# A three-block network in one launch: queries of the first attention padded by map, its small loads moved to SyncE, and the second pool gate moved behind mixing

## The chip, the cores and the metric

The kernel runs on one core of a Trainium2 chip. The metric is device time in microseconds for one execution. Engines are called TensorE (PE, with its weight loads as PEld), VectorE (DVE), ScalarE (ACT), GpSimd (POOL) and SyncE (SP).

## The reference

One input of 256 tokens by 1024 features goes through two blocks of a first network and one block of a second. What matters here is the first network's start:

```python
def adaln_params(cond, w_mod, b_mod):
    m = jax.nn.silu(cond) @ w_mod + b_mod
    return jnp.split(m, N_MOD, axis=-1)          # shift, scale, gate, twice

# block 0: differential attention, 8 heads of 2 maps x 64, latents (256) attend to context + latents (512)
hx, hc = modulate(x, sh1, sc1), modulate(h_ctx, csh1, csc1)
k_c, v_c = project_kv(hc, w_qkv)
q_l = apply_rope(project_q(hx, w_qkv), cos, sin)
k_l, v_l = project_kv(hx, w_qkv);  k_l = apply_rope(k_l, cos, sin)
s = jnp.einsum('bqhmd,bkhmd->bhmqk', q * (HEAD_DIM ** -0.5), k)   # m: the two maps
p = jax.nn.softmax(s, axis=-1)
a = p[:, :, 0] - lam * p[:, :, 1]
o = jnp.einsum('bhqk,bkhe->bqhe', a, v)
...
# block 1: pooled means over windows of 2, 4, 8, 16 tokens, then a matmul for each group
y = jnp.einsum('bsgi,gio->bsgo', pooled, w_pool).reshape(B, S, D)
y_lat = y * pool_scale
# both blocks
x = layer_norm(ALPHA * x + g1 * y_lat, ln_g[i, 0], ln_b[i, 0])
x = layer_norm(ALPHA * x + g2 * swiglu(modulate(x, sh2, sc2), ffn_w_in, ffn_w_out), ln_g[i, 1], ln_b[i, 1])
```

The second network's block (three attention branches and an FFN) follows and isn't touched.

## The kernel before

All matrix products with large weights run as three matmuls in fp32r: each operand is split in a high part and a low remainder, and `mm3` (lines 77 to 80) adds high x high, high x low and low x high. Weights come from HBM by SyncE into four `raw` buffers; `wsplit` lets ScalarE cast a half of a unit (line 70) and VectorE subtract (line 71). PSUM has four banks called mm, two called tp (transposes) and two called s (`sbank`). A tile framework orders the instructions of each engine before the launch from its own estimates: it takes what is ready and comes first in the program, and `behind(ins)` only adds the rule that what the block holds stands behind `ins` where both are on one engine.

**The modulation stream.** The modulation vectors of the later stages come from 4 MB slices of w_mod. `mod_stream` is a generator: one step (`mod_step`) loads 512 KB by GpSimd (line 131, three `mraw` buffers) and lets VectorE multiply it by the condition and add it to `acc` (line 132). Eight steps make a group. Behind the eighth, TensorE sums `acc` over partitions, into columns (line 138) or, for a gate, into rows with two matmuls by a matrix of ones (line 145), which ScalarE copies back (line 146). The groups come in the order f0 (two groups), g1_0, p (two), f1 (two), g2_0, g1_1, g2_1; `mod_until(key)` runs steps until that key is there. The layer norm's rows (`ln_rows`, line 345) and `pool_scale` use the same `mraw` buffers.

**The first attention.** The first modulation comes in four quarters q: `load_quarter` issues two pieces of w_mod, the columns of x and ctx and the rows of w_qkv for the first head pair on SyncE's queue; `mod_quarter` and `modulate` make the modulated, transposed hT (latents) and hc (context); `Chunk.products` adds the quarter's part of keys, queries and values of head pair 0. `rest(q)` holds the products that come later, the last being `rest(3)`. Then come, behind the last modulation activation (`seq["mod"]`, line 567), ScalarE's DMA issues for prow (norm gains in rows), rope (the tables) and lamr (lines 642 to 658), the transpose of prow (line 648) and the small sums for lambda. For each of four head pairs g: `rope_T` rotates keys and then queries on VectorE (lines 684 to 687), transposes them (line 690) and splits them in high and low parts (`split_to`, lines 673 and 674). The two maps of a head lie on partitions 0 to 63 and 64 to 127. `scores` makes one set of scores for one query tile and one head:

```python
for i, (q, k) in enumerate(((qh, kh), (qh, kl), (ql, kh))):
    for m in range(2):
        p = slice(m * 64, (m + 1) * 64)
        with behind(*last):
            last = pe.matmul(Sm[m], q[p, h, tk], k[p, h, :], start=i == 0, stop=i == 2).ins,
```

So each matmul reads 64 partitions, and maps alternate. VectorE takes minima (line 708), ScalarE exponentials (line 710), VectorE mixes the maps (line 713), TensorE transposes (line 717). After each of the four sets two modulation steps stand behind the mixing. The projections of the next head pair are what TensorE does meanwhile.

**The pool stage.** The first FFN takes three modulation steps for each pair of hidden tiles and one for each unit of its output, which leaves two steps of g1_1. `mod_until("g1_1")` runs these, then `psg` is loaded and multiplied with the gate's rows (lines 839 to 841), then the FFN's held-back output products go through the norm n2 (line 254 and on), are mixed over tokens by matmuls (line 837) and scaled and shifted into T (line 870); `project_T` multiplies by the pool's weights (line 882), and the norm n3 multiplies the product by psg. The bias table of the second network (`bias_tables`, line 159) is filled by GpSimd at the start of this stage.

## Time and profile before

| | |
|---|---|
| median of 3 runs | 1156.4 us (1154.62 to 1157.67) |
| profiled execution | 1157.81 us, of which the span of the trace is 1156.0 us |
| TensorE busy | 1129.1 us (98% of the span) |
| VectorE busy | 829.0 us (72%) |
| ScalarE busy | 575.8 us (50%) |
| mean granted TensorE clock | 0.995 of full speed |

Busy time is the time in which an engine has an instruction of its own under way; register, semaphore and DMA-issuing instructions don't count. Matmuls overlap: each record is longer than the distance to the next one, so the cost of a stream of matmuls is read from starts. The granted clock is the share of TensorE's full 2.4 GHz; 0.50 is the other level, 1.2 GHz.

### The profile page before, as it was taken

How to read it: one execution, taken by the hardware profiler on the slowest of the kernel's cores; microseconds unless marked ns; L12 is line 12 of the kernel's file. 1: busy time of each engine (PE TensorE's matmuls, PEld its weight loads, DVE VectorE, ACT ScalarE, POOL GpSimd, SP SyncE). 2: the span in 40 equal slices, each digit the busy share in tenths (PEclk: the TensorE clock that was granted, in tenths of full speed). 3: DMA queues.
4: the chain of work that ended last, by engine and by line, in shares of the span. 5: the costliest groups of instructions: out<-in, count | busy, mean ns of one | idle time of the engine just before them, and what ended most of it. 6: DMA issues, size and time to landing. Idle time of an engine off the chain costs nothing. (4 is left out here: it accounts for less than half of the span.)

```text
span 1156.0 us, 19870 instructions
## 1 busy us (share of the span) xinstructions
PE 1129.1 (98%) x7967; PEld 1035.3 (90%) x7967; DVE 829.0 (72%) x1547; ACT 575.8 (50%) x1017; POOL 83.9 (7%) x154
## 2 busy tenths in 40 slices
PE   8989999999999999999999889999999999999998
PEld 7979988889999877999988779989999989999986
DVE  5677887887887877856654779788788674655541
ACT  5643444576444436654543655455346356545430
POOL 0101110100111111000000020000100000000000
PEclk9999999999999999999999999999999999999999
DMA  9956545648998993867565353660456254664530
GB/s 311 324 174 212 183 155 174 219 146 285 313 317 291 341 353 121 249 217 257 210 222 175 109 180 121 179 200 29 146 160 223 77 178 147 219 199 167 215 113 37
DMA packets 149098, 229.69 MB, mean 199 GB/s; under 512 B 5708, under 2 KB 121051, under 8 KB 149006
## 3 DMA queue, kind: packets, MB, share of 16 engines
q1 hardware_dynamic: 133440, 176.10, 46.6%
q0 software_dynamic: 14672, 50.63, 13.0%
q10 hardware_dynamic: 894, 1.69, 0.5%
q8 instruction: 63, 1.03, 0.4%
q14 instruction: 29, 0.24, 0.1%
HBM read 226.36 MB, written 2.04 MB: 198 GB/s over the span
## 5 line engine op out<-in xcount | busy, mean ns | idle before, releaser
L71 DVE TENSOR_TENSOR wlo<-raw,whi 128x1024 fp32r<-128x1024 f32 (+2 forms) x318 | 372.7, 1193 | 135.2 <-ACT whi L70 133.7
L70 ACT CAST whi<-raw 128x1024 fp32r<-128x1024 f32 (+2 forms) x318 | 316.3, 1028 | 229.6 <-PE mm L80 86.7
L78 PE MATMUL mm<-hTh,whi 128*128 128x256 f32 x1056 | 299.1, 283 | 0.0
L80 PE MATMUL mm<-hTh,wlo 128*128 128x256 f32 x1056 | 298.9, 283 | 0.0
L79 PE MATMUL mm<-hTl,whi 128*128 128x256 f32 x1056 | 298.3, 282 | 0.0
L79 PEld LDWEIGHTS mm<-hTl,whi 128*128 128x128 f32 x1056 | 199.4, 189 | 0.3
L78 PEld LDWEIGHTS mm<-hTh,whi 128*128 128x128 f32 x1056 | 199.3, 189 | 0.3
L80 PEld LDWEIGHTS mm<-hTh,wlo 128*128 128x128 f32 x1056 | 199.3, 189 | 0.1
L78 PE MATMUL mm<-whi,hTh 128*128 128x256 f32 (+4 forms) x592 | 185.5, 314 | 2.3 <-DVE hTh L336 1.8
L80 PE MATMUL mm<-whi,hTl 128*128 128x256 f32 (+4 forms) x592 | 184.8, 313 | 0.4 <-DVE hTl L337 0.4
L79 PE MATMUL mm<-wlo,hTh 128*128 128x256 f32 (+4 forms) x592 | 184.3, 312 | 0.6 <-DVE wlo L71 0.6
L78 PEld LDWEIGHTS mm<-whi,hTh 128*128 128x128 f32 x592 | 112.4, 190 | 9.0 <-DVE hTh L336 2.9
L79 PEld LDWEIGHTS mm<-wlo,hTh 128*128 128x128 f32 x592 | 112.3, 190 | 4.9 <-DVE wlo L71 1.0
L80 PEld LDWEIGHTS mm<-whi,hTl 128*128 128x128 f32 x592 | 111.9, 189 | 5.2 <-DVE hTl L337 1.0
L132 DVE SCALAR_TENSOR_TENSOR acc<-mraw,csil,acc 128x1024 f32<-128x1024 f32 x80 | 102.2, 1280 | 10.0 <-DMA mraw<-in_w_mod_dram 9.6
L78 PE MATMUL mm<-whi,hid 128*128 128x512 f32 x264 | 104.3, 395 | 0.0
L79 PE MATMUL mm<-wlo,hid 128*128 128x512 f32 x264 | 104.2, 395 | 0.0
L80 PE MATMUL mm<-whi,hid 128*128 128x512 f32 x264 | 103.7, 393 | 0.0
L131 POOL DMA_DIRECT2D mraw<-in_w_mod_dram x80 | 42.6, 533 | 367.8 <-DVE acc L132 269.8
L79 PEld LDWEIGHTS mm<-wlo,hid 128*128 128x128 f32 x264 | 49.6, 188 | 11.6 <-issue 1.0
L80 PEld LDWEIGHTS mm<-whi,hid 128*128 128x128 f32 x264 | 49.6, 188 | 11.5 <-issue 0.7
L78 PEld LDWEIGHTS mm<-whi,hid 128*128 128x128 f32 x264 | 49.6, 188 | 11.4 <-issue 0.7
(329 smaller groups left out, 1556.6 us busy)
## 6 DMA issues: line engine op xcount, KB each, us to landing
raw<-in_ffn_w_in_dram SPq DMA_DIRECT2D x44, 1024.0 KB, 7.1
mraw<-in_w_mod_dram POOLq DMA_DIRECT2D x80, 512.0 KB, 5.0
raw<-in_ffn_w_out_dram SPq DMA_DIRECT2D x22, 1024.0 KB, 4.9
raw<-in_w_ffn_in_dram SPq DMA_DIRECT2D x22, 1024.0 KB, 5.2
raw<-in_w_in_dram SPq DMA_DIRECT2D x16, 1024.0 KB, 5.5
raw<-in_w_ffn_out_dram SPq DMA_DIRECT2D x11, 1024.0 KB, 5.0
raw<-in_w_in_dram SPq DMA_DIRECT2D x14, 768.0 KB, 4.4
raw<-in_attn_w_qkv_dram SPq DMA_DIRECT2D x9, 1024.0 KB, 8.4
```

The lines of the kernel that those rows point to most:

```text
L70: se.copy(hv[:, sl], raw[:, sl])
L71: seq["sub"] = ve.tensor_sub(lv[:, sl], raw[:, sl], hv[:, sl].bitcast(F32)).ins
L78: pe.matmul(o, lh, rh, start=first, stop=False, **kw)
L79: pe.matmul(o, lh, rl, start=False, stop=False, **kw)
L80: return pe.matmul(o, ll, rh, start=False, stop=last, **kw).ins
L131: gp.dma_start(raw, wv[:, k, g * 1024:(g + 1) * 1024])
L132: ve.scalar_tensor_tensor(acc, raw, csil[:, k, 0:1], acc, op0=ALU.mult, op1=ALU.add)
```

## The change

The queries of a head pair lie in two tiles QZ (high and low part) with one plane for each map; the partitions of the other map are zeros that GpSimd writes once. A score matmul then reads all 128 partitions of queries and keys, and the set runs map by map, three matmuls each. The query split is done for 64 partitions at a time. Two of the eight modulation steps of a head pair stand behind the query rotation, one behind the mixing of each set, two ahead of the head output. The small loads (prow, rope, lamr) are issued by SyncE behind the last load of quarter 3, and their users stand behind `rest(3)` and the last fill of weights. In the pool stage the last steps of g1_1, its sums and psg stand behind mixing.

```diff
--- before.py
+++ after.py
@@ -25,7 +25,7 @@
 QS = -0.125
 HALF = (slice(0, 512), slice(512, 1024))
 
-STEPS_S, STEPS_IN, STEPS_OUT = 2, 3, 1
+STEPS_S, STEPS_IN, STEPS_OUT = 1, 3, 1
 
 
 @with_exitstack
@@ -523,7 +523,7 @@
             rw = wp.tile([128, 2048], F32, tag="raw", name="raw", bufs=4)
             rw = rw[:, :1536].rearrange("p (w k c) -> p w k c", w=3, k=2)
             for i, kind in enumerate((1, 0, 2)):
-                sp.dma_start(rw[:, i], wq[:, 2 * q:2 * q + 2, kind * 1024:kind * 1024 + 256])
+                seq["ld"] = sp.dma_start(rw[:, i], wq[:, 2 * q:2 * q + 2, kind * 1024:kind * 1024 + 256]).ins
                 if i == 1:
                     load_x("ctx", q)
             return raws, rw
@@ -603,11 +603,12 @@
                         tk = slice(t * 128, (t + 1) * 128)
                         for k in ks:
                             if self.kind == 1:
-                                mm3(self.PC[:, t, :], wh[:, k, tk], wl[:, k, tk], hc[0][:, k, :], hc[1][:, k, :],
+                                i = mm3(self.PC[:, t, :], wh[:, k, tk], wl[:, k, tk], hc[0][:, k, :], hc[1][:, k, :],
                                     k == 0 and t == 0, k == 7, **kw)
                             else:
-                                mm3(self.PC[:, t, :], hc[0][:, k, tk], hc[1][:, k, tk], wh[:, k, :], wl[:, k, :],
-                                    k == 0 and t == 0, k == 7, **kw)
+                                i = mm3(self.PC[:, t, :], hc[0][:, k, tk], hc[1][:, k, tk], wh[:, k, :], wl[:, k, :],
+                                        k == 0 and t == 0, k == 7, **kw)
+                    return i
 
         ALLK = range(8)
         ck, cq, cv = (Chunk(kind, 0) for kind in (1, 0, 2))
@@ -616,11 +617,25 @@
         def rest(q):
             ks = range(2 * q, 2 * q + 2)
             cv.products(ks, con=False)
-            ck.products(ks, lat=False)
+            seq["rest"] = ck.products(ks, lat=False)
 
         for q in range(4):
             with behind(*((first_dma.ins,) if not q else ())):
                 raws, rw = load_quarter(q)
+            if q == 3:
+
+                with behind(seq["ld"]):
+                    prow = cp.tile([128, 128], F32, name="prow")
+                    gp.memset(prow, 0.0)
+                    sp.dma_start(prow[32:64], I["ln_g"].rearrange("l w (k c) -> (l w k) c", c=128))
+                    sp.dma_start(prow[64:96], I["ln_b"].rearrange("l w (k c) -> (l w k) c", c=128))
+                    sp.dma_start(prow[96:104], rows128(I["norm1_g_2"][0]))
+                    sp.dma_start(prow[104:112], rows128(I["norm2_g_2"][0]))
+                    sp.dma_start(prow[112:113], I["attn_subln_g"])
+                    rope = at.tile([128, 2, 2, 2, 64], F32, name="rope")
+                    sp.dma_start(rope, I["k_rope"].rearrange("(t p) v w c -> p t v w c", p=128))
+                    lamr = at.tile([128, 256], F32, tag="aT", name="lamr", bufs=5)
+                    sp.dma_start(lamr, I["attn_lambda"].rearrange("a b c -> a (b c)").to_broadcast([128, 256]))
             mod_quarter(q, raws)
             if not q:
                 keep_busy(6, seq["mc"])
@@ -636,14 +651,7 @@
         oT = [oc.tile([128, 2048], F32R, tag="oT" + i, name="oT", bufs=1).rearrange("p (k c) -> p k c", k=8)
               for i in ("hi", "lo")]
 
-        with behind(seq["mod"]):
-            prow = cp.tile([128, 128], F32, name="prow")
-            gp.memset(prow, 0.0)
-            se.dma_start(prow[32:64], I["ln_g"].rearrange("l w (k c) -> (l w k) c", c=128))
-            se.dma_start(prow[64:96], I["ln_b"].rearrange("l w (k c) -> (l w k) c", c=128))
-            se.dma_start(prow[96:104], rows128(I["norm1_g_2"][0]))
-            se.dma_start(prow[104:112], rows128(I["norm2_g_2"][0]))
-            se.dma_start(prow[112:113], I["attn_subln_g"])
+        with behind(seq["mod"], seq["rest"], *seq["fill"]):
             pcol_ps = sbank()
             pe.transpose(pcol_ps[:, :128], prow, ident)
             pcol = cp.tile([128, 128], F32, name="pcol")
@@ -652,10 +660,6 @@
             LG = lambda l, w: pcol[:, 32 + (l * 2 + w) * 8: 40 + (l * 2 + w) * 8]
             LB = lambda l, w: pcol[:, 64 + (l * 2 + w) * 8: 72 + (l * 2 + w) * 8]
             N1, N2 = pcol[:, 96:104], pcol[:, 104:112]
-            rope = at.tile([128, 2, 2, 2, 64], F32, name="rope")
-            se.dma_start(rope, I["k_rope"].rearrange("(t p) v w c -> p t v w c", p=128))
-            lamr = at.tile([128, 256], F32, tag="aT", name="lamr", bufs=5)
-            se.dma_start(lamr, I["attn_lambda"].rearrange("a b c -> a (b c)").to_broadcast([128, 256]))
 
             lsum = at.tile([128, 4], F32, name="lsum")
             ljunk = at.tile([128, 64], F32, name="ljunk")
@@ -673,8 +677,7 @@
             se.copy(hi, src)
             ve.tensor_sub(lo, src, hi.bitcast(F32))
 
-        def rope_T(P, hi, lo, v):
-
+        def rope_T(P, v):
 
             cos, sin = rope[:, :, v, 0, None, :], rope[:, :, v, 1, None, :]
             r12 = at.tile([128, 2, 512], F32, tag="e", name="r12", bufs=4)
@@ -684,26 +687,28 @@
             ve.tensor_mul(rv, pv, cos.to_broadcast([128, 2, 4, 64]))
             ve.tensor_mul(r2v[:, :, :, 0:32], pv[:, :, :, 32:64], sin[:, :, :, 0:32].to_broadcast([128, 2, 4, 32]))
             ve.tensor_mul(r2v[:, :, :, 32:64], pv[:, :, :, 0:32], sin[:, :, :, 32:64].to_broadcast([128, 2, 4, 32]))
-            ve.tensor_add(r12[:, 0, :], r12[:, 0, :], r12[:, 1, :])
+            seq["rope"] = ve.tensor_add(r12[:, 0, :], r12[:, 0, :], r12[:, 1, :]).ins
             b = tbank()
             for i in range(4):
                 pe.transpose(b[:, i * 128:(i + 1) * 128], r12[:, 0, i * 128:(i + 1) * 128], ident)
-            split_to(hi, lo, b.rearrange("p (t h c) -> p t h c", t=2, h=2))
-
-        def scores(qh, ql, kh, kl, h, t, sm):
+            return b.rearrange("p (t h c) -> p t h c", t=2, h=2)
+
+
+        QZ = [at.tile([128, 2, 2, 256], F32R, name=f"QZ{i}") for i in range(2)]
+        for a in QZ:
+            for m in range(2):
+                gp.memset(a[(1 - m) * 64:(2 - m) * 64, m].bitcast(F32), 0.0)
+
+        def scores(kh, kl, h, t, sm):
 
 
             tk = slice(t * 128, (t + 1) * 128)
             mx = at.tile([128, 6], F32, tag="mx", name="mx", bufs=4)
             e = at.tile([128, 2, 512], F32, tag="e", name="e", bufs=4)
             Sm = [sbank(), sbank()]
-
-            last = ()
-            for i, (q, k) in enumerate(((qh, kh), (qh, kl), (ql, kh))):
-                for m in range(2):
-                    p = slice(m * 64, (m + 1) * 64)
-                    with behind(*last):
-                        last = pe.matmul(Sm[m], q[p, h, tk], k[p, h, :], start=i == 0, stop=i == 2).ins,
+            for m in range(2):
+                for i, (q, k) in enumerate(((QZ[0], kh), (QZ[1], kh), (QZ[0], kl))):
+                    pe.matmul(Sm[m], q[:, m, h, tk], k[:, h, :], start=i == 0, stop=i == 2)
             for m in range(2):
                 ve.tensor_reduce(mx[:, m:m + 1], Sm[m], axis=AX.X, op=ALU.min)
             for m in range(2):
@@ -758,12 +763,16 @@
                 ck.products(ALLK)
                 cq = Chunk(0, g)
                 cq.products(ALLK)
-            qhl = [at.tile([128, 2, 256], F32R, tag=f"q{i}", name=f"q{i}", bufs=1) for i in range(2)]
             khl = [at.tile([128, 2, 512], F32R, tag=f"k{i}", name=f"k{i}", bufs=1) for i in range(2)]
             lat = lambda a: a.rearrange("p h (t c) -> p t h c", t=2)
-            rope_T(ck.PL, *[lat(a[:, :, 256:512]) for a in khl], 0)
+            split_to(*[lat(a[:, :, 256:512]) for a in khl], rope_T(ck.PL, 0))
             split_to(khl[0][:, :, 0:256], khl[1][:, :, 0:256], ck.PC)
-            rope_T(cq.PL, *[lat(a) for a in qhl], 1)
+            qT = rope_T(cq.PL, 1)
+            for m in range(2):
+                p = slice(m * 64, (m + 1) * 64)
+                split_to(*[lat(a[p, m]) for a in QZ], qT[p])
+            with behind(seq["rope"]):
+                mod_step(2)
             if not g:
                 cv.products(ALLK, lat=False)
                 vt = values(cv)
@@ -771,13 +780,15 @@
             sm = at.tile([128, 4, 2], F32, tag="sm", name="sm", bufs=2)
             for t in range(2):
                 for h in range(2):
-                    aTs[t, h] = scores(*qhl, *khl, h, t, sm[:, 2 * t + h, :])
+                    aTs[t, h] = scores(*khl, h, t, sm[:, 2 * t + h, :])
                     with behind(seq["mix"]):
                         mod_step(STEPS_S)
             if g:
                 cv = Chunk(2, g)
                 cv.products(ALLK)
                 vt = values(cv)
+            with behind(seq["mix"]):
+                mod_step(2)
             head_out(aTs, vt, g, sm)
 
 
@@ -825,7 +836,7 @@
         f.rest(hT, STEPS_IN, 2)
         o2 = f.out(I["ffn_w_out"][0], 2, STEPS_OUT)
 
-        mod_until("g1_1")
+        mod_until("p")
         Ap, Bp = mods["p"]
         pm = hp.tile([128, 2, 4, 256], F32, tag="hTh", name="pm", bufs=1)
         se.dma_start(pm, I["k_pool"].rearrange("(t p) g c -> p t g c", p=128))
@@ -836,11 +847,9 @@
             rg = bands[t]
             pe.matmul(dst[:, rg], lhs, pm[:, t, q, rg], start=first, stop=t == 1, skip_group_check=True)
 
-        psg = pools["ap"].tile([128, 1024], F32, tag="mraw", name="psg", bufs=3)
-        gp.dma_start(psg, I["pool_scale"].to_broadcast([128, 1024]))
-        ve.tensor_mul(psg, psg, mods["g1_1"])
         rows = ln_rows(0, 1)
         n2 = Norm()
+        mod_until("g2_0")
         for t in range(2):
             for n in range(2):
                 with behind(mods["mm"]):
@@ -869,9 +878,12 @@
         for k in range(8):
             ve.scalar_tensor_tensor(T[:, k, :], M[k // 2][:, k % 2, :], Ap[:, k:k + 1], shift[:, k, :], op0=ALU.mult,
                                     op1=ALU.add)
+        mod_until("g1_1")
+        psg = pools["ap"].tile([128, 1024], F32, tag="mraw", name="psg", bufs=3)
+        gp.dma_start(psg, I["pool_scale"].to_broadcast([128, 1024]))
+        ve.tensor_mul(psg, psg, mods["g1_1"])
         with behind(n2.scaled[1]):
             n2.residual(0, rows)
-        mod_until("f1")
         n3 = Norm()
         hT = h_tiles()
         B = [[bank() for n in range(2)] for t in range(2)]
```

## Rows read from the trace of the kernel before

**Rows 1.** The page, part 1: busy us (share of the span) and instructions
```profile
PE 1129.1 (98%) x7967; PEld 1035.3 (90%) x7967; DVE 829.0 (72%) x1547; ACT 575.8 (50%) x1017; POOL 83.9 (7%) x154
```

**Rows 2.** Windows: busy us (instructions) of each engine, granted clock, DMA share, GB/s
```profile
58.60:66.90 8.30, 5.08 (x42) 4.71 (x41) 4.31 (x15) 4.52 (x7) 0.00 (x0) 1.00 0.62 167
66.90:70.30 3.40, 3.40 (x18) 3.40 (x17) 3.40 (x6) 1.43 (x3) 0.00 (x0) 0.50 0.02 5
72.20:98.00 25.80, 25.50 (x187) 21.83 (x188) 24.40 (x37) 11.31 (x24) 3.71 (x7) 1.00 0.74 243
```

**Rows 3.** Timeline: start, us, instruction, count, [idle before <-releaser]
```profile
59.51 0.30 PE L648 MATMUL s<-idsel,prow 128*128 128x128 f32 x1 [0.67 <-DMA prow<-in_norm_g_dram]
...
61.78 0.69 DVE L684 TENSOR_TENSOR r<-mm,rope 128x512 f32<-128x512 f32 x1 [1.63 <-DMA rope<-in_k_rope_dram]
...
65.94 0.65 PE L690 MATMUL tp<-idsel,r 128*128 128x128 f32 x4 [2.55 <-DVE r L687]
```

**Rows 4.** Timeline and page part 6: loads and their neighbours
```profile
38.69 0.56 SPq L54 DMA_DIRECT2D raw<-in_attn_w_qkv_dram  x1
...
53.21 0.32 ACTq L642 DMA_DIRECT2D prow<-in_ln_g_dram  x1
...
55.73 0.48 ACTq L658 DMA_DIRECT2D lamr<-in_attn_lambda_dram  x1
...
57.93 1.05 ACT L70 CAST whi<-raw 128x1024 fp32r<-128x1024 f32 x1
...
59.85 0.29 DVE L650 COPY pcol<-s 128x128 f32<-128x128 f32 x1 [4.49 <-PE s L648]
...
raw<-in_attn_w_qkv_dram SPq DMA_DIRECT2D x9, 1024.0 KB, 8.4
```

**Rows 5.** Timeline of TensorE: one score set in pieces, one whole
```profile
75.47 0.28 PE L80 MATMUL mm<-whi,hTl 128*128 128x256 f32 x1
75.68 0.50 PE L706 MATMUL s<-k,q 64*128 64x512 f32 x1
...
76.66 0.96 PE L706 MATMUL s<-k,q 64*128 64x512 f32 x5
...
77.77 0.28 PE L79 MATMUL mm<-wlo,hTh 128*128 128x256 f32 x1
77.89 0.28 PE L80 MATMUL mm<-whi,hTl 128*128 128x256 f32 x1
...
195.74 1.23 PE L706 MATMUL s<-k,q 64*128 64x512 f32 x6
...
197.12 0.28 PE L79 MATMUL mm<-wlo,hTh 128*128 128x256 f32 x1
```

**Rows 6.** Timeline of TensorE, first and last of 29 matmuls with 512 columns
```profile
414.04 0.39 PE L80 MATMUL mm<-whi,hid 128*128 128x512 f32 x1
...
420.39 0.40 PE L78 MATMUL mm<-whi,hid 128*128 128x512 f32 x1
```

**Rows 7.** Lines 673 and 674: ns min/median/max, first and last start, form
```profile
L673 ACT CAST q<-tp x4: 585/586/588, 71.6 to 195.1; 128x512 fp32r<-128x512 f32 x4
...
L674 DVE TENSOR_TENSOR q<-tp,q x4: 691/692/692, 72.2 to 195.7; 128x512 fp32r<-128x512 f32 x4
```

**Rows 8.** Timeline of the pool stage; DMA issues from 400 to 460 us
```profile
419.64 0.53 POOL L840 DMA_DIRECT2D psg<-in_pool_scale_dram  x1 [2.94 <-DVE acc L132]
...
425.87 1.96 PE L145 MATMUL s<-acc,ones 128*128 128x512 f32 x4 [0.17 <-issue]
...
438.79 0.18 POOL L159 MEMSET tab<- 33x112 f32 x1 [5.54 <-PE mm L80]
...
443.95 1.19 PE L837 MATMUL tp<-pm,z 128*128 128x136 f32 x8 [1.28 <-ACT z L281]
...
448.46 0.68 DVE L254 TENSOR_TENSOR z<-mm,psg 128x512 f32<-128x512 f32 x1
...
mraw<-in_w_mod_dram POOLq DMA_DIRECT2D x7, 512.0 KB, 6.2
```

## The prediction

> **What bounds the kernel now.** I began with the page's busy shares: TensorE is busy 98% of the span, VectorE 72%, ScalarE 50%, GpSimd 7% [rows 1]. The kernel is TensorE-bound, so an edit counts if it takes matmul time away, fills a hole in TensorE, or opens one. Then I asked for busy times in stretches around the change [rows 2]. The reader is to see three things. From 58.6 to 66.9 us, where the first attention begins, TensorE has holes: 5.08 us busy of 8.30. In the next stretch, 66.9 to 70.3 us, it is busy throughout, but at half the granted clock, the 1.2 GHz level. From 72.2 to 98 us it is nearly full (25.50 of 25.80), and VectorE hardly less so (24.40). Then I read the timeline of the holes [rows 3]: TensorE waits 0.67 us at 59.51 for a load into prow, and 2.55 us at 65.94 for the rotated keys; VectorE could begin that rotation only at 61.78, when rope had landed. ScalarE issues these loads behind the last modulation activation, seven in a row from 53.21 to 55.73 [rows 4]. Last I read the timelines of the score matmuls [rows 5] and of the second pool gate [rows 8].
>
> **Part one: the score matmuls.** There are 16 score sets (4 head pairs, 2 query tiles, 2 heads) of six matmuls of 512 columns; now each matmul uses 64 PE rows. What does a set cost TensorE? Its two maps need two banks that the set before is still reading, so 12 sets come in two pieces, 1 matmul and then 5, with three projection matmuls between. From the projection matmul at 75.47 to the one at 77.77 there are 2.30 us [rows 5]. Five 256-column matmuls start in that stretch (one before the first piece, three between, one behind). Such a matmul takes 0.12 us undisturbed (77.77 to 77.89), so the set takes 2.30 - 0.59 = 1.71 us. The first set of a head pair comes whole: from 195.74 to 197.12 are 1.38 us, less one matmul behind it (0.12), plus the late start that a piece has (0.21 from 75.47 to 75.68 instead of 0.12): 1.35 us. All 16: 12 x 1.71 + 4 x 1.35 = 25.9 us.
>
> After the change a set is six matmuls of 512 columns over 128 rows, three for one map, then three for the other. The trace has none like it on the score banks. The nearest rows are the 512-column matmuls with 128 rows and the same number format in the first FFN, three of which also follow each other in one bank: 28 steps from 414.04 to 420.39, 0.227 us each [rows 6]. A set is then 1.36 us, in one piece or two, and 16 sets are 21.8 us. Saved: 4.1 us. Bounds: 0, if pieces still pay at their edges; 4.1, as no row shows such a matmul faster. I take 4.1, since the rows on both sides of the subtraction are of the same kind.
>
> At this place the Trainium skill speaks against the change. Its page "TensorE: Matmul & The Clock Gate" (part 3, "The mechanism") says that matmuls on different row groups run at the same time, a pair in about the time of one, and recommends it for short contractions. By that rule a set now costs three matmul times, an estimate of 0.7 us, 10.9 us for all, and doubling the rows adds 10.9 us where I subtract 4.1. The rows do not bear that price out: whatever the pairs do inside, a set costs 1.35 to 1.71 us [rows 5].
>
> **What it adds.** Queries now lie padded by map, so their split is done in two halves of 64 partitions. One split is now an ACT cast of 0.586 us and a DVE subtraction of 0.692 us [rows 7]; a half has as many elements in each partition and should take as long. So each of 4 head pairs gets one more of both, 2.3 us of ScalarE and 2.8 us of VectorE in all, just ahead of its first score set. With nothing to cover them that is 5.1 us; where projection matmuls cover them, 0. TensorE's holes between 72.2 and 98 us are 0.3 us in all [rows 2], so cover is there now, and I take 0.1 a head pair: +0.4 us. The zeros of the padded tiles are four GpSimd fills; with 7% of the span busy [rows 1] it has room. If its loads stood behind them, one w_mod load would be late, with two others in store.
>
> **Part two: the small loads.** SyncE issues them behind the last quarter's loads, at about 38.7 us [rows 4]. Their issues took ScalarE some 3.0 us (53.21 to the end of the last, 56.2), so SyncE's next load, weights of the second head pair, is issued about 3 us later, at 41.7. Such a load lands 8.4 us after its issue [rows 4], so at about 50 instead of 47. Its first reader is the cast at 57.93, so 7 us of other work cover the delay; beyond that the casts would move one for one. The small loads land by about 50 us too. VectorE ends its work on the last quarter 4.49 us before 59.85, at 55.4 [rows 4], so the rotation starts there instead of at 61.78, 6.4 us sooner. The waits of 0.67 and 2.55 us go. With the hole gone, the stretch at half clock behind it should go too: it holds 18 matmuls in 3.40 us [rows 2], 0.19 us each against 0.12, so 1.3 us are lost in it (0 if the clock falls anyway, 1.7 if half of the stretch counts). Sum: 4.5 us; bounds 0 to 4.9.
>
> What is late next? VectorE, with the splits, two modulation steps that now stand there, and the weight splits of the second head pair, without which TensorE has no cover. It starts 6.4 us sooner and has 0.7 us more to do: a lead of 5.7. TensorE wants to be 4.5 us sooner, and by the end of this head pair 3 x 0.35 for its split sets more: 5.6 us. Just enough.
>
> **Part three: the steps spread.** A head pair keeps eight modulation steps: two behind the rotation, four among the scores, two at the end. VectorE's sum stays the same, so the cost is 0, as long as TensorE has projections to do meanwhile. Without that cover, two steps ahead of the query split delay the first scores by some 2.5 us; that bound belongs to the first rival.
>
> **Part four: the second gate.** The last two of its eight steps and its sums over partitions now come behind mixing. Now the sums take 1.96 us of TensorE at 425.87, with matmuls waiting; later, before 443.95, TensorE idles 1.28 us until rows are normalised [rows 8]. Sums that wait until then can fill that hole: -1.3 us. But the product of pool_scale and gate, needed at 448.46, gets late. Of three load buffers the layer norm rows hold two, so the two loads of the steps (6.2 us each), two steps (1.3), the pool_scale load (as long) and the product (1.2) go one after another: 22.4 us from 419.64, where a buffer came free, to 442.0. That leaves 6 us. Bounds -1.3 and +16 (rivals); I take -0.8, as the sums' copies also meet a ScalarE at work on the shift.
>
> **The sum.** -4.1 + 0.4 - 4.5 - 0.8 = -9.0 us. The profiled execution took 1157.8 us (span 1156.0), which gives 1148.8. It is 1.4 above the median of the runs, 1156.4, so against the median 1147.4 us.
>
> **The rivals.**
> *VectorE takes over the first pair's stall.* For: 24.40 of 25.80 us [rows 2], and a margin of 0.1 us above. Against: TensorE still has the context's value products, 48 matmuls, as cover. The 4.5 us come back as waits for split weights or queries, less 0.3: 1151.6 us. Chance 0.17.
> *The score sets save nothing,* as the second split and the order by map put waits where the pieces' edges were: 3.7 us lost, 1151.1 us. Against: TensorE is full of projection work from 72 us on. Chance 0.10. Both together, or small loads that land too late: 1155 to 1156, no change. Chance 0.04.
> *Slower: GpSimd's queue.* In the program the gate's last loads stand behind the fills of the bias table, which wait until 438.79 [rows 8]. If GpSimd keeps that order, the loads start at about 441 and the product comes at 463.4 instead of 448.5. TensorE then idles up to 14.9 us, with another 1.3 at half clock: 1147.4 + 0.8 + 16.2 = 1164.4 us. It is slower than now from a product at about 455.4 on (448.5 + 8.2 - 1.3). Against: at 419.64 GpSimd loaded as soon as a buffer was free. Chance 0.06.
> *By the packing rule* the scores cost 10.9 + 4.1 us more than I forecast: 1162.4 us. The measured sets speak against it; chance 0.02.
> *More than forecast:* the second splits stay covered (-0.4), the gate's product costs nothing (-0.5), the whole slow stretch comes back (-0.4), and TensorE's small holes, 0.3 us in 26 [rows 2], close until the attention ends at 210 (-1.6): 1144.5 us. Chance 0.08.
> The forecast has 0.53, its own range 1145 to 1150.
>
> **The numbers.** A change within 0.3% (3.5 us) can't be told from none here. Faster by more, below 1152.9: the forecast, the better case and four fifths of the two 1151 cases, 0.83. Slower by more: 0.07. The rest is 0.10. The range 1143 to 1153.5 leaves out the slower cases and no change, and adds at either end a part of the 3 us over which the runs before spread.
>
> **What would show it.** Right: score matmuls of 128 rows 0.22 to 0.23 us apart, no lengthened matmul behind a set; no wait for prow or rope; the rotation at about 55 us; full clock at 67 us; the gate's sums near 442. Wrong: a wait of over 1 us before the first score set of each pair; VectorE without a gap and TensorE waiting for it before 98 us; the pool product later than the z it goes into.

## The result and the profile after

The change made the kernel slower: 1164.4 us (median of 4 runs, 1162.5 to 1165.1) against 1156.9 for four runs of the kernel before, a ratio of 1.0051 with an interval of 1.0031 to 1.0072. Ratios here and below are those on record, with their 95% intervals, and differences in us that stand beside a ratio are taken from it; the ratio of two medians can differ from it by up to 0.14% (here it is 1.0065). One run of twelve of a later kernel, the loads with the score sets, took 2829.5 us and is left out of its ratio. The forecast was 1147.4 us, with 0.83 on faster. The profiled execution took 1162.46 us with a span of 1160.6. It is the quickest of the four, so the traces show 4.6 us of span between the kernels where the medians show 7.5.

The busy shares hide it. This is part 1 of the page after, which answers to [rows 1]:

```profile
PE 1130.6 (97%) x7967; PEld 1044.7 (90%) x7967; DVE 831.3 (72%) x1551; ACT 579.5 (50%) x1021; POOL 86.1 (7%) x158
```

TensorE does the same work in a longer span. So the same three stretches as in [rows 2], busy time of each engine, then the granted clock:

```profile
58.60:66.90 8.30, 8.14 (x65) 7.54 (x63) 7.23 (x11) 6.96 (x10) 1.07 (x2) 1.00 0.96 318
66.90:70.30 3.40, 3.12 (x20) 2.79 (x21) 3.34 (x5) 2.81 (x6) 0.00 (x0) 1.00 0.58 189
72.20:98.00 25.80, 25.80 (x211) 25.10 (x210) 23.60 (x48) 11.59 (x29) 4.62 (x8) 1.00 0.69 217
```

The start of the attention went as forecast: TensorE is busy for 8.14 us of 8.30 where it had been for 5.08, the next stretch is at the full clock (2.4 GHz) instead of half, and from 72.2 to 98 us there is no hole at all. The timeline of that place says why (start, us, instruction; answers to [rows 3, 4]):

```profile
38.67 0.41 SPq L630 DMA_DIRECT2D prow<-in_ln_g_dram  x1
...
43.88 0.47 SPq L638 DMA_DIRECT2D lamr<-in_attn_lambda_dram  x1
44.53 9.35 SPq L54 DMA_DIRECT2D raw<-in_attn_w_qkv_dram  x4
...
55.45 0.68 DVE L687 TENSOR_TENSOR r<-mm,rope 128x512 f32<-128x512 f32 x1
...
58.82 0.27 PE L656 MATMUL s<-idsel,prow 128*128 128x128 f32 x1
...
58.92 0.60 PE L693 MATMUL tp<-idsel,r 128*128 128x128 f32 x4
58.94 1.05 ACT L70 CAST whi<-raw 128x1024 fp32r<-128x1024 f32 x1 [0.76 <-PE mm L79]
```

The rotation begins at 55.45 us (forecast 55.4), and neither prow nor the rotated keys are waited for. SyncE pays more than forecast for its seven loads, 5.86 us (38.67 to 44.53) instead of about 3, and the cast that needs the next weights still starts at 58.94 without waiting for them.

The score sets and the second split (timeline of TensorE; then one row each of lines 677 and 678, ns min/median/max; answer to [rows 5, 7]):

```profile
104.29 0.62 PE L711 MATMUL s<-k,QZ 128*128 128x512 f32 x2
104.75 0.28 PE L78 MATMUL mm<-whi,hcT 128*128 128x256 f32 x1
...
105.43 0.50 PE L711 MATMUL s<-k,QZ 128*128 128x512 f32 x1 [0.17 <-ACT QZ L677]
105.76 0.28 PE L78 MATMUL mm<-whi,hcT 128*128 128x256 f32 x1
...
109.78 1.36 PE L711 MATMUL s<-k,QZ 128*128 128x512 f32 x5
110.97 0.27 PE L722 MATMUL tp<-idsel,e 128*128 128x128 f32 x1
```

```profile
L677 ACT CAST QZ<-tp x8: 579/580/582, 60.8 to 193.2; 64x512 fp32r<-64x512 f32 x8
...
L678 DVE TENSOR_TENSOR QZ<-tp,QZ x8: 673/687/695, 63.2 to 193.8; 64x512 fp32r<-64x512 f32 x8
```

A half split does take as long as a whole one. In an undisturbed run a score matmul takes 0.23 to 0.24 us (104.29 to 104.75 for two, 109.78 to 110.97 for five; forecast 0.227), but the one at 105.43, which had waited for the second half's split, takes 0.33.

At 235.65 us, where TensorE ends the attention's last product (240.46 before), the kernel is 4.8 us ahead. The forecast had 8.2 there. This lead, and more, is lost in the pool stage. Timeline of VectorE, then of GpSimd, then of TensorE (answer to [rows 8]):

```profile
422.56 1.28 DVE L132 SCALAR_TENSOR_TENSOR acc<-mraw,csil,acc 128x1024 f32<-128x1024 f32 x1 [4.68 <-DMA mraw<-in_w_mod_dram]
428.54 1.28 DVE L132 SCALAR_TENSOR_TENSOR acc<-mraw,csil,acc 128x1024 f32<-128x1024 f32 x1 [4.69 <-DMA mraw<-in_w_mod_dram]
...
430.88 0.68 DVE L254 TENSOR_TENSOR z<-mm,acc 128x512 f32<-128x512 f32 x1
...
452.65 1.22 DVE L884 TENSOR_TENSOR psg<-psg,acc 128x1024 f32<-128x1024 f32 x1 [1.62 <-ACT acc L146]
```

```profile
407.85 0.53 POOL L345 DMA_DIRECT2D lng<-in_ln_g_dram  x1 [2.94 <-DVE acc L132]
411.32 0.53 POOL L345 DMA_DIRECT2D lnb<-in_ln_b_dram  x1 [2.94 <-DVE acc L132]
414.79 0.53 POOL L131 DMA_DIRECT2D mraw<-in_w_mod_dram  x1 [2.94 <-DVE acc L132]
424.14 0.53 POOL L131 DMA_DIRECT2D mraw<-in_w_mod_dram  x1 [8.83 <-DVE acc L132]
```

```profile
431.38 0.39 PE L80 MATMUL mm<-whi,hid 128*128 128x512 f32 x1
438.54 2.18 PE L848 MATMUL tp<-pm,z 128*128 128x136 f32 x8 [6.77 <-ACT z L281]
...
446.43 1.19 PE L848 MATMUL tp<-pm,z 128*128 128x136 f32 x8 [1.13 <-ACT z L281]
...
450.12 1.88 PE L145 MATMUL s<-acc,ones 128*128 128x512 f32 x4
...
460.49 1.72 PE L320 MATMUL tp<-idsel,z 128*128 128x128 f32 x8 [0.62 <-ACT z L281]
```

The reader is to follow it from load to hole. GpSimd loads the two layer norm rows first, at 407.85 and 411.32, and they keep two of the three buffers until the residual. So the gate's last two loads share the third: the second is issued only at 424.14, when the first step has read the buffer. In the program the two steps stand behind mixing, but the framework's order on VectorE has them ahead of the norm's first addition (L254). VectorE waits 4.68 us, then 4.69 us, for their loads and reaches the norm at 430.88; with the layer norm rows loaded last (below) it does so at 425.72. TensorE starts the last of the second FFN matmul's products at 431.38 and has nothing from 431.77 to 438.54. The windows show what the hole does to the clock, some 10 us at the half level (1.2 GHz):

```profile
434.00:444.30 10.30, 5.76 (x25) 5.76 (x26) 4.24 (x14) 4.76 (x11) 2.21 (x4) 0.50 0.38 120
```

The first mixing, 32 matmuls, takes 6.8 us (438.54 to 445.3), nearly all of it in this stretch. And the gate's sums at 450.12 are not in the hole. They stand in the middle of the projection, because both s banks, the only ones that they may use, hold mixed rows until VectorE has read them.

### The profile page after: what moved, and what is told of

Its sections match the earlier page's. It is cut to its first block, busy times and chain, and to the rows that moved or that the text cites. A ratio compares the mean times of both kernels' runs of the same rounds, so it can differ in the third digit from the quotient of the medians.

```text
span 1160.6 us, 19896 instructions
## 1 busy us (share of the span) xinstructions
PE 1130.6 (97%) x7967; PEld 1044.7 (90%) x7967; DVE 831.3 (72%) x1551; ACT 579.5 (50%) x1021; POOL 86.1 (7%) x158
## 6 DMA issues: line engine op xcount, KB each, us to landing
raw<-in_attn_w_qkv_dram SPq DMA_DIRECT2D x9, 1024.0 KB, 10.6
```

## The experiments

Ratios are to runs of the kernel before on the same chip. The four parts were first taken apart: loads by SyncE, score sets, steps spread, gate.

**The gate left where it was** (all else as in the change; the steps, the sums and the product ahead of mixing, as before):

```
-        mod_until("p")
+        mod_until("g1_1")
...
+        psg = pools["ap"].tile([128, 1024], F32, tag="mraw", name="psg", bufs=3)
+        gp.dma_start(psg, I["pool_scale"].to_broadcast([128, 1024]))
+        ve.tensor_mul(psg, psg, mods["g1_1"])
         rows = ln_rows(0, 1)
         n2 = Norm()
-        mod_until("g2_0")
...
-        mod_until("g1_1")
...
```

> The changed kernel with the pool gate back at its old place (steps, sums and psg ahead of the norm n2). Theory A (the loss is made in the pool stage alone, by two modulation steps that stand ahead of the norm on VectorE and wait 4.7 us each for loads; the attention's part gains the 4.8 us by which the second stage starts sooner): about 1152 us, 5 us under before. Theory B (the attention's part is what costs, the pool stage only shows it): not under 1157. Theory C (all gains are real, 8.2 us as forecast, and something between 240 us and the pool stage ate 3.4): about 1149.

Measured: 1153.89 us, ratio 0.9957 (0.9941 to 0.9974), near the first of its three cases. The attention ends at the same 235.64 us, and ahead of the second mixing there is the old wait, 1.16 us. So the gate's move makes the whole loss: without it the change is a gain.

**The gate alone** (only the lines above, the other way round, on the kernel before):

> The kernel before with nothing but the gate moved behind mixing. Theory A: the pool stage turns a lead of 4.8 us into a lag of 4.8 in the traces, so the move costs about 9.6 us: 1166.5, with TensorE idle over 5 us before the first mixing matmul and some 5 us lost at half clock. Theory B: within 2 us of before.

Measured: 1166.52 us, ratio 1.0076 (1.0057 to 1.0095), some 8.8 us slower. The timeline of VectorE has the same two waits:

```profile
426.10 1.29 DVE L132 SCALAR_TENSOR_TENSOR acc<-mraw,csil,acc 128x1024 f32<-128x1024 f32 x1 [4.99 <-DMA mraw<-in_w_mod_dram]
...
432.52 1.29 DVE L132 SCALAR_TENSOR_TENSOR acc<-mraw,csil,acc 128x1024 f32<-128x1024 f32 x1 [5.13 <-DMA mraw<-in_w_mod_dram]
```

TensorE then idles 6.97 us to 442.5, and the clock is at half for 10.2 us. The loss is there without any other part.

**The layer norm rows loaded last** (the changed kernel, one line moved; TensorE's order stays the same):

```
-        rows = ln_rows(0, 1)
         n2 = Norm()
...
         ve.tensor_mul(psg, psg, mods["g1_1"])
+        rows = ln_rows(0, 1)
```

> The changed kernel, with the loads of the layer norm rows issued behind psg instead of ahead of the gate's last two steps, so that these find two buffers free and no longer share one. TensorE's order is that of the changed kernel. Theory A: VectorE's two waits of 4.7 us shrink to what they were before (0.8 and 3.1) and the 6.8 us hole before mixing closes: about 1151 us, 13 under the changed kernel. Rival (the sums and the product behind mixing are themselves what delays TensorE, not the loads): within 3 us of the changed kernel, 1161 to 1165.

Measured: 1155.58 us, ratio 0.9979 (0.9966 to 0.9992). VectorE's waits, and what is left for TensorE:

```profile
417.09 1.28 DVE L132 SCALAR_TENSOR_TENSOR acc<-mraw,csil,acc 128x1024 f32<-128x1024 f32 x1 [1.78 <-DMA mraw<-in_w_mod_dram]
419.98 1.28 DVE L132 SCALAR_TENSOR_TENSOR acc<-mraw,csil,acc 128x1024 f32<-128x1024 f32 x1 [1.61 <-DMA mraw<-in_w_mod_dram]
...
443.72 1.23 DVE L883 TENSOR_TENSOR psg<-psg,acc 128x1024 f32<-128x1024 f32 x1 [1.63 <-ACT acc L146]
```

```profile
432.37 1.19 PE L848 MATMUL tp<-pm,z 128*128 128x136 f32 x8 [0.73 <-ACT z L281]
...
441.18 1.88 PE L145 MATMUL s<-acc,ones 128*128 128x512 f32 x4
```

With three buffers for the steps' loads the waits shrink from 4.7 to 1.8 and 1.6 us, the hole from 6.77 to 0.73, and the kernel is no longer slower than before: the ratio falls from 1.0051 to 0.9979, 0.72% or 8.3 us. So the buffer shared by the two loads is the main cause. The expectation was 13 us. Against the run with the gate in its old place (0.9957) 0.22%, or 2.5 us, is still missing, which is within the two intervals. The gate's move still gains nothing: its sums stand in the projection, and the 2 us by which mixing is earlier than with the gate in its old place (438.3 against 440.3 for VectorE's first read of it) are gone when ScalarE begins to scale the third norm's rows (450.7 against 450.2).

**The steps held back behind the norm** (the changed kernel):

```
-        mod_until("g1_1")
+        with behind(n2.scaled[1]):
+            mod_until("g1_1")
```

> The changed kernel with the gate's last two steps ordered behind the norm's last scaling on VectorE; the shared buffer stays. Theory A: mixing starts without the hole, but now the second load begins only when the first step has run at about 437, so the product of pool_scale and gate comes some 8 us after the z it goes into: 1158 to 1162 us, the hole now ahead of the norm n3. Rival (the position on VectorE does not matter, the late loads delay all the same): 1164 or more.

Measured: 1160.92 us, ratio 1.0017 (1.0003 to 1.0031). The hole goes from the second norm and comes back ahead of the third, since the product pool_scale x gate is now late, at 447.60 us (timeline of TensorE):

```profile
443.55 1.95 PE L145 MATMUL s<-acc,ones 128*128 128x512 f32 x4
...
455.44 1.97 PE L320 MATMUL tp<-idsel,z 128*128 128x128 f32 x8 [4.22 <-ACT z L281]
```

Half clock follows from 453.3 on, for 6.8 us. The loads in series cost something in both places where they were tried.

**The loads alone** (the block of seven loads moved to SyncE behind the last quarter, their users placed as in the change, on the kernel before):

```
+            if q == 3:
+                with behind(seq["ld"]):
...
+                    sp.dma_start(prow[32:64], I["ln_g"].rearrange("l w (k c) -> (l w k) c", c=128))
...
-            se.dma_start(prow[32:64], I["ln_g"].rearrange("l w (k c) -> (l w k) c", c=128))
```

> The kernel before with nothing but the small loads moved to SyncE. Theory D (the attention's whole gain of 4.8 us in the trace is the closed holes and the clock; the score part gives nothing): 4.5 to 5 us under before, 0.996, without the waits for prow and for the rotated keys. Theory E (the forecast's split: loads 4.5, scores 3.7 less losses elsewhere): also 4.5 here, so the runs below tell them apart. Rival (VectorE takes the stall over): 2 us or less.

Measured: 1152.94 us, ratio 0.9949 (0.9935 to 0.9962), 5.9 us faster (the medians lie 5.0 apart). The attention ends at 235.47 us, no later than with all parts together (235.65).

**The score sets alone** (padded queries, 128 rows, two half splits, on the kernel before):

```
...
-            for i, (q, k) in enumerate(((qh, kh), (qh, kl), (ql, kh))):
-                for m in range(2):
-                    p = slice(m * 64, (m + 1) * 64)
-                    with behind(*last):
-                        last = pe.matmul(Sm[m], q[p, h, tk], k[p, h, :], start=i == 0, stop=i == 2).ins,
+            for m in range(2):
+                for i, (q, k) in enumerate(((QZ[0], kh), (QZ[1], kh), (QZ[0], kl))):
+                    pe.matmul(Sm[m], q[:, m, h, tk], k[:, h, :], start=i == 0, stop=i == 2)
...
```

> The kernel before with nothing but the padded queries, the scores on 128 rows map by map and the split in halves; steps stay two behind each set. Theory D (a set still pays: 0.233 us a matmul, 0.33 for the first one behind a wait or a transpose, and 1.9 us of waits for the second split over four head pairs): no change, within 1.5 us of before. Theory E: 3.7 us under before. Packing rule: some 10 us over.

Measured: 1163.72 us, ratio 1.0042 (1.0028 to 1.0056), 4.9 us slower, which none of its three cases had. The attention ends at 244.97 us, 4.5 us later than before, although the sets themselves cost a little less (25.3 us, counted as in the next section, against 26.7). TensorE waits 3.00 us for the rotated keys (2.55 before) and later 1.53 us for a modulation step ahead of a group's sums:

```profile
66.60 0.66 PE L689 MATMUL tp<-idsel,r 128*128 128x128 f32 x4 [3.00 <-DVE r L686]
...
99.48 0.72 PE L138 MATMUL s<-ones,acc 128*128 128x1 f32 x5 [1.53 <-DVE acc L132]
```

Beside the stretch at half clock behind the first wait, which the kernel before has too, there are two more (windows, as in [rows 2]):

```profile
102.20:105.60 3.40, 3.40 (x19) 3.40 (x18) 2.82 (x9) 1.99 (x2) 0.74 (x2) 0.50 0.65 214
143.20:146.60 3.40, 3.40 (x19) 3.40 (x18) 3.40 (x9) 1.14 (x8) 1.20 (x2) 0.50 0.39 146
```

All of this stands outside the sets, so the loss is made of waits and slow matmuls there. That the second split's work makes VectorE late is likely, but no run takes the split out.

**The spread alone** (two of eight steps behind the rotation, four among the scores, two at the end, on the kernel before):

```
-STEPS_S, STEPS_IN, STEPS_OUT = 2, 3, 1
+STEPS_S, STEPS_IN, STEPS_OUT = 1, 3, 1
...
+            with behind(seq["rope"]):
+                mod_step(2)
...
+            with behind(seq["mix"]):
+                mod_step(2)
```

> The kernel before with nothing but the 32 modulation steps spread. Forecast and theory D: no change, within 1.5 us. Rival (two steps ahead of the query split delay the first scores of each head pair): up to 2.5 us a pair, 5 to 10 us over before.

Measured: 1158.23 us, ratio 1.0000 (0.9990 to 1.0010). It costs nothing and gives nothing by itself.

**The 64-row matmuls map by map** (the kernel before with its two loops exchanged, so that matmuls of the two maps alternate only at the border between them):

```
-            for i, (q, k) in enumerate(((qh, kh), (qh, kl), (ql, kh))):
-                for m in range(2):
-                    p = slice(m * 64, (m + 1) * 64)
+            for m in range(2):
+                p = slice(m * 64, (m + 1) * 64)
+                for i, (q, k) in enumerate(((qh, kh), (qh, kl), (ql, kh))):
```

> The kernel before with the six score matmuls of a set in the new order, map by map, still on 64 rows each and without padding. It separates the order from the rows. If pairs on the two row halves overlap now (a pair every 0.33 us or less) and the order ends that, a set grows from 1.16 us to six times 0.23 or more, 1.4 to 2 us: 16 sets 3 to 12 us over before. If the order's gain (no piece of one matmul) outweighs it: no change or up to 3 us under before.

Measured: 1168.3 us, ratio 1.0083 (1.0068 to 1.0098). The 16 sets cost TensorE some 32 us instead of 26.7; the rest of the 9.6 us lies outside them. Only 12 of the 96 matmuls still start within 0.1 us of the one before, where 36 did. So in the kernel before the two maps' matmuls did overlap. What that is worth is worked out in the next section.

**The loads with the spread, and the loads with the score sets** (two kernels, each with the blocks shown above):

> The kernel before with the small loads on SyncE and the 32 steps spread, and nothing else. If the spread costs nothing (as it did alone) and the loads give 0.5%: 1152 to 1153 us, 0.995. If the spread is worth something only beside the earlier rotation: under 1151.

> The kernel before with the small loads and the padded scores, the steps two behind each set as before. It tells why the scores cost 5 us alone and about 1 us in company. If the scores' loss comes from the steps that stand in VectorE's way where they were (a hole of 1.5 us at 98 us and two stretches at half clock): 3 to 5 us over the loads alone, 1156 to 1158. If it came from the hole at 64 us that the loads close: as with loads, scores and spread, 1153 to 1154.

Measured: loads and spread 1153.90 us, ratio 0.9966 (0.9952 to 0.9980); loads and score sets 1155.22, ratio 0.9971 (0.9958 to 0.9984). Neither is better than the loads alone, and the first was expected at 0.995. The second lies between its two cases, so it does not settle why the score sets lose 4.9 us alone: the closed first hole takes about half of it away. Without the spread the score sets bring back a wait for a step among the attention's work (timeline of TensorE), and a half clock from 94.0 us behind it:

```profile
91.31 1.95 PE L138 MATMUL s<-ones,acc 128*128 128x1 f32 x16 [1.43 <-DVE acc L132]
```

With the spread this wait is gone. That is what the spread is for; in the times, 0.9971 without it and 0.9957 with it, its gain is within the intervals.

**The gate's sums put into the hole** (loads alone; the steps stay in place, the layer norm rows are loaded last, and the sums get a bank of the mm pool right behind the first mixing):

```
...
+                        last = mix(S[q // 2][:, q % 2, :], u, q, ones, u == 0 and q % 2 == 0)
...
+                seq["row"] = bank
+                with behind(last):
+                    mod_until("g1_1")
+                seq["row"] = sbank
...
```

> Loads alone, and the gate's sums put into the hole ahead of the second half of the mixing: steps where they were, layer norm rows loaded last, sums in an mm bank, since both s banks hold mixed rows until T is made. If the hole can hold the sums (1.2 us) and the product is not late: 1 to 1.5 us under the loads alone, 1151.5. If the copies and the product, now among ScalarE's shifts and VectorE's T, set the end of this stage: no change against the loads alone, or 1 us over.

Measured: 1152.93 us, ratio 0.9954 (0.9937 to 0.9970). The timeline of TensorE shows the sums where the wait had been, and the second mixing at once behind them; below it the loads alone at the same place:

```profile
433.14 2.02 PE L841 MATMUL mm<-pm,ones 128*128 128x136 f32 x16
435.00 1.88 PE L145 MATMUL mm<-acc,ones 128*128 128x512 f32 x4
436.71 1.09 PE L841 MATMUL tp<-pm,z 128*128 128x136 f32 x8
```

```profile
435.63 2.02 PE L841 MATMUL mm<-pm,ones 128*128 128x136 f32 x16
438.93 1.19 PE L841 MATMUL tp<-pm,z 128*128 128x136 f32 x8 [1.28 <-ACT z L281]
```

ScalarE begins to scale the third norm's rows 1.5 us earlier than with the loads alone (448.13 against 449.59), and the profiled span is 1.0 us shorter (1149.6 against 1150.6). But 0.7 us of that is there before the sums: the attention's last product ends at 234.79 against 235.47, and the trace of the loads alone has a stretch at half clock from 9.7 to 13.1 us that the other has not. So the traces leave about 0.8 us for the sums, and the times do not tell the two kernels apart. They are the quickest of the study by their medians.

## Why the prediction was wrong

**The ledger.** On the profiled execution the forecast was 1148.8 us, and 1162.46 was measured, 13.7 us more. The attention's end was to be 8.2 us ahead and is 4.8 ahead: 3.4 us. From there to the third norm the forecast was -0.8 us, and the lead of 4.8 became a lag of 5.0 (ScalarE begins to scale the third norm's rows at 459.62 against 454.61): +9.8, that is 10.6 us over the forecast. Together 14.0, of which 0.4 comes back by the end.

**Part four, the second gate, is the step that failed:** "Bounds -1.3 and +16 (rivals); I take -0.8". Measured alone it is +8.8 us. The working saw that three loads and two steps would go one after another through one buffer, and it compared the end of that series with the time at which the *product* is needed. What it did not ask is who stands behind the waiting steps on VectorE. The norm does, so the price falls some 12 us before the product is due: TensorE runs dry at 431.77, and the kernel with the loads alone uses the product first at 443.44. When the FFN's products end, the changed kernel is 7.0 us ahead (431.6 against 438.6, 1.9 of it the sums taken out), and at the third norm it is 5.0 behind, 12.0 us in all. TensorE's rows give 11.3 of them: the hole 6.8; the first mixing at half clock, 6.8 instead of 4.0 us in the kernel with the loads alone (433.68 to 437.65), 2.8; the sums in the projection 1.7 (450.12 to 451.83). The experiment with the rows loaded last takes the hole and the half clock away again by moving two loads that nobody needed yet.

The gain itself, sums in the hole, was also misplaced: the step took for granted that TensorE could run them there. Their banks were taken, and they ran at 450.12, 3.7 us after the second mixing that they should have preceded. With a free bank they fit, and the second mixing then starts 2.2 us earlier than with the loads alone (436.71 against 438.93); of the 1.3 us forecast for that, about 0.8 is left at the third norm.

**The rival for a slower kernel had the price and not the place.** It gave 1164.4 us for loads that GpSimd issues too late behind its fills. GpSimd issued them at 414.79 and 424.14, before the fills, and the product was not what TensorE waited for first. So the time is right by luck, by another path; no case of the forecast was this one, and with it the range, 1143 to 1153.5, missed by 10.9 us.

**Part one, the score sets, was mis-sized:** -4.1 us forecast, and the sets cost TensorE as much as before. Counted in the trace from the start of each score matmul to the start of the next matmul, and with what the neighbours of a piece start late, 16 sets were 26.7 us before (forecast 25.9) and are 26.9 after (forecast 21.8). Of the 26.9, 96 matmuls at 0.233 make 22.4; 23 of them take 0.30 to 0.34, 16 of these the first behind a wait or behind the transposes of the attention weights, another 2.1; one takes 0.71; and the pieces start late by 1.9, part of it in waits for the second split. So the forecast's row, matmuls that follow each other in one bank, was right for what it showed, and the sets are not such a run: they come in 34 pieces. The rival "the score sets save nothing", with a chance of 0.10, held in its number. The run of the score sets alone lost 4.9 us, by waits for VectorE and half clock outside the sets, near the bound of 5.1 that the forecast gave for splits without cover; that the splits are the reason is not shown.

**The pairs of 64-row matmuls.** In the kernel before 36 pairs of matmuls, one of each map, start a few ns apart, most of them 3 or 4; the other 24 matmuls, those of the single pieces and the last of each piece of five, have no partner. In a piece of five the first pair takes 0.33 us to the next start and the second 0.23. That is as long as one matmul on 128 rows (0.233), or one on 64 rows in the middle of a map's three (0.236 in the kernel map by map). At the end of a piece 0.32 to 0.43 us go by. So the pairs did overlap, which the Trainium skill states in "TensorE: Matmul & The Clock Gate", part 3, "The mechanism"; that a pair takes the time of one is borne out by the second pair in a piece of five, and by no other. Over all 96 matmuls two cost 20.4 / 48 = 0.43 us, where two on 128 rows cost 0.52, and two on 64 rows map by map 0.53 (25.6 us for 96). The rival that rested on that rule gave 1162.4 us, near what was measured, but its 10.9 us were to be spent in the score sets, where nothing was: in pieces of one and five matmuls too few pairs run at the price of one. The overlap's gain of 4.6 us (25.0 less 20.4 for the 96) was eaten by the pieces' edges, the late starts at either side of a piece: 6.3 us in 28 pieces, 0.22 each, against 1.9 in 34 after the change. The Trainium skill's "TensorEngine Tiling (Array Packing)", "Key Properties", says that a change of tiling mode drains TensorE; the dear edges of the 64-row pieces agree with it, though no run here took the edge apart. Trading overlap for edges is what the change does, and it comes out even.

**Part two, the loads, was right:** -4.5 us forecast, -5.9 measured alone (0.9949), and 5.0 at the attention's end in that trace (235.47 against 240.46). The wait for prow, the wait for the keys and the half clock at 67 us all went, and the delay of SyncE's weight loads, twice as long as forecast, stayed covered. **The second split** made TensorE wait 0.31 us at the first pair and 0.16 to 0.17 at each of the others, near the 0.1 taken. **Part three, the spread,** cost 0 as forecast. **VectorE taking over the first pair's stall** did not happen: TensorE is full from 72 to 98 us.

**What stays open.** The differences among the loads alone, with the spread, and with the score sets and the spread (0.9949, 0.9966, 0.9957) are within their intervals, and whether the sums in the hole beat the loads alone is not settled by the times. Nor is it settled what makes the score sets alone 4.9 us slower, and whether some 2.5 us of the gate's cost remain when the rows are loaded last.

## What to carry to other kernels

When a step that waits for a load is moved, look first at what stands behind it on its own engine, and only then at who needs its result; the first price comes due earlier. Count the buffers that are free at the new place, and load last what is needed last: two rows loaded 37 us before their first use cost this kernel 8 us. A matmul's price taken from a long run holds only inside a run; for work that is cut into pieces, price the pieces' edges and first matmuls from rows.

## What the hardware showed that was not expected

Of the holes followed here, the longer had the longer stretches at half clock. The wait of 2.55 us that ended at 65.94 before the change had 3.4 us at half clock [rows 2, 3]; 4.22 us of idling had 6.8 us, and 6.77 and 6.97 us had 10.2 us each, beginning within the hole. The wait of 1.28 us in the kernel before [rows 8] had none right behind it, while one of 1.53 us with the score sets alone had 3.4 us. A hole is not the whole account: from 456.0 to 459.4 us the kernel before is at half clock with TensorE busy for all of the 12 us ahead, and with the loads alone the same place is at the full clock.

The half clock also spread to a neighbour. In the changed kernel ScalarE's first copy of shift waits 3.67 us for the slow mixing, and the second tile's statistics stand behind it on ScalarE, so VectorE waits 4.02 us. TensorE therefore waits for the second mixing's rows as long as it did before (1.13 us against 1.28), though it comes to them later (timelines of ScalarE and VectorE):

```profile
444.38 0.47 ACT L877 ACTIVATE shift<-mm,Bp 128x256 f32<-128x256 f32 x1 [3.67 <-PE mm L848]
444.75 0.19 ACT L266 ACTIVATE nc<-nc 128x1 f32<-128x1 f32 x1
...
444.98 0.16 DVE L267 RECIPROCAL nc<-nc 128x1 f32<-128x1 f32 x1 [4.02 <-ACT nc L266]
```
